# A decoder layer in split float32 on one core: two of seven Strassen operands formed later, half of the input's norm on GpSimd, the last product in two passes, no padded blocks in attention

## The chip, the cores and the metric

One core of a Trainium2 chip. The metric is device time in microseconds of one execution of the whole program. Rows of the profile come from one profiled execution. Engines: PE is TensorE (PEld its weight loads), DVE is VectorE, ACT is ScalarE, POOL is GpSimd, SP is SyncE, which here only issues DMAs.

## The reference

A decoder layer on 1024 tokens of width 1024 with 16 meta tokens ahead of them, all in float32:

```python
h = concatenate([meta, x])
h = h + 0.5 * rms_norm(swiglu(rms_norm(h, g_ffn1_pre), w_ffn1_in, w_ffn1_out), g_ffn1_post)
u = rms_norm(h, g_mix_pre)
q, k, v, f_logit, c_b, c_c, c_in, gate_a, gate_c = split_cols(u @ w_in)
# 8 heads of 64, causal, logits q.k/8 + F[t] - F[s], F = cumsum(log_sigmoid(f_logit + b_forget))
y_attn = forgetting_attention(q, k, v, log_f) @ w_attn_branch
y_conv = (c_b * short_conv(c_c * c_in, conv_w)) @ w_conv_branch
mixed = (sigmoid(gate_a) * y_attn + sigmoid(gate_c) * y_conv) @ w_out
h = h + rms_norm(mixed, g_mix_post)
h = h + 0.5 * rms_norm(swiglu(rms_norm(h, g_ffn2_pre), w_ffn2_in, w_ffn2_out), g_ffn2_post)
return h[16:]
```

`swiglu(x, w_in, w_out)` is `(silu(a) * b) @ w_out` with `a, b` the halves of `x @ w_in`; the hidden width is 2816, 22 tiles of 128.

## The kernel before, in words

**Numbers.** Every float32 operand is split into a high part `h`, rounded to the fp32r format by a ScalarE copy, and a low part `l`, the rest, by a VectorE subtraction (`split_into`, L138). A product is three matmuls, h·h, h·l and l·h, accumulated in PSUM (`mm3`, L142 to L146). So most matmuls of the trace stand on lines 144 to 146 and most vector work on lines 139 and 140, whatever the stage; the tiles' names tell the stage.

**Strassen products.** The two feed-forward blocks multiply by a scheme of seven products of half size (Strassen-Winograd). The input side has the operands B11, B21 (the first half of the tokens, first and second half of the channels), B22 (second half) and the sums T1 to T4. T2, T3 and T1 are differences of B22, B12 and B11; T4 = B21 - T2.

**Opening of the first block** (L389 to L456). Nine blocks of tokens come in (block 0 is the 16 meta tokens, 1 to 4 the first half, 5 to 8 the second). `norm_x` (L414) squares and sums on ScalarE (L421), takes the power -1/2 on GpSimd (L188), multiplies by the norm and the gain on VectorE (L426, two operations of 512 columns per block) and transposes on TensorE (L429) into two PSUM banks. For blocks 5 to 8 `sums_split` (L240) copies the second bank out (L252), forms the sums on VectorE (L253 to L256) and puts T2, T3, T1, then T4 (L261, L262) and B22 as h and l into their slots, block by block. The transposes of these four blocks share two PSUM banks (`psS`), so a block's transposes wait until the T1 and T3 of the one before are read.

**`ffn_in`** (L270) runs the 22 tiles. `first` makes P1 and P2 with B11 and B21; for tiles 0 to 2 it runs ahead of everything else. `rest` (L344) forms the tile's weight sums on VectorE (`load_rest`, L316) and makes P6 with T2, P7 with T3, P5 with T1, calls `late()` if there is one and this is tile 0 (L357), then makes P4 with T4 and P3 with B22. P1, P2, P6 and P4 of the first block also take the 16 meta tokens: 24 matmuls of 264 columns; P7, P5 and P3 are 12 of 512.

**Opening of the second block** (L1022 to L1067). The output projection of the mixer runs in two halves of tokens; the second half goes through `sums_split` with `t4=False`, and T4 is formed whole in `late` (L1057), two channel pairs at a time, when tile 0 reaches it.

**Attention** (L897 to L978). Per head, the queries are taken as four pairs of 128. `softmax` (L897) makes the weights of one tile of queries; for the first of a pair it sets the 128 columns behind its last key to zero (L918, GpSimd), so that both have the same length. `values` (L921) takes two key blocks of both query tiles at a time: four transposes of 128x128 into a bank (L935), the split, and per key block two matmuls of 256 columns (L943, L945), h and l. Other matmul work, gates and branches, is woven in between (`fill_work`).

**The last product** (L1147 to L1184). The second feed-forward block's output is again seven products, here with the tokens on the output side. P4 is the last: 11 steps in 6 batches; `prep2` (L1102) loads A's raw part and B's raw part, forms B's difference with a running sum R (L1121), and splits both. 11 x 4 x 3 = 132 matmuls of 512 columns fill four accumulators, `drain2` (L1145) adds them to the output, and `finish` (L1163) takes four tiles of 128 tokens: load the residual into one of two buffers `hr` (L1168), square and sum (L1171), scale (L1174), add (L1176, two halves), store.

**Order.** The program is written in order of data; the framework orders each engine's instructions by a simulated schedule with priorities (blocks under `tc.high_priority()` first). Each engine then runs its own list in that order, and SP and ACT issue their DMAs in order.

Of the kernel before, what the change touches and what calls it, by code (L numbers as in the profile page):

```python
# [13 lines left out]
P = 128  # L14
D = 1024
# [52 lines left out]
def hybrid_layer(ctx, tc, x, meta, w_in, b_forget, conv_w, w_attn, w_conv, w_out,  # L68
# [171 lines left out]
    def sums_split(bk, pt, e, ca, cb, t4=True):  # L240


        at = lambda b: bk[b].at(ALLP, ALLP, cb if b in ("T1", "T3", "B22") else ca)
        t1, t3 = pt
        b22, t2 = e

        def put(b, src):
            d = at(b)
            split_into(d.h, d.l, src)

        b11, b21 = at("B11"), at("B21")
# [4 lines left out]
        V.tensor_sub(t2, b22, t1)  # L256
# [149 lines left out]
    SLOTS = {"B11": (0, 1), "B21": (2, 3), "T2": (4, 5), "T3": (6, 7), "T1": (8, 9), "T4": (10, 11), "B22": (12, 13)}  # L406
# [7 lines left out]
    def norm_x(i):  # L414
# [9 lines left out]
        for q in range(2):  # L424
# [13 lines left out]
    for b in ("T2", "T3", "T1", "T4", "B22"):  # L438
        bk1[b] = operand(SLOTS, b, META, "u1")

# [17 lines left out]
    ffn_in(bk1, META, w1_in, g1d, loc, psD, psS, ahead, "w")  # L458
# [438 lines left out]
    def softmax(h, qt, fb):  # L897
# [19 lines left out]
        if qt % 2 == 0:  # L917
            G.memset(p[:, nk:nk + P], 0.0)  # L918
        return p

    def values(h, qp, pr, v):  # L921
# [97 lines left out]
    SLOTS2 = {"B11": (4, 5), "B21": (9, 0), "T3": (12, 6), "B22": (3, 10), "T4": (13, 11)}  # L1019
    bk2 = {b: operand(SLOTS2, b, 0, "u2") for b in ("B11", "B21")}  # L1020
    bk2["T1"], bk2["T2"] = mix[0, 0], mix[0, 1]
    for c, half in enumerate(TH):  # L1022
        if c:
            for b in ("T3", "B22"):
                bk2[b] = operand(SLOTS2, b, 0, "u2")

# [13 lines left out]
        def leave(i, w):  # L1040
# [6 lines left out]
            else:  # L1047
                sums_split(bk2, pts, halves(w[0]), cs, cs, t4=False)
# [6 lines left out]
    bk2["T4"] = operand(SLOTS2, "T4", 0, "u2")  # L1055

    def late():  # L1057
        for k in range(0, 4, 2):
            ks = slice(k, k + 2)
            t = loc["s"].page(f"t4_{k}")[:, :D].rearrange("p (k t) -> p k t", k=2)  # L1060
            b21, t2, t4 = (bk2[b].at(ALLP, ks) for b in ("B21", "T2", "T4"))
            V.tensor_sub(t, f32(b21.h), f32(t2.h))
            V.tensor_add(t, t, f32(b21.l))
            V.tensor_sub(t, t, f32(t2.l))
# [143 lines left out]
```

## Time and profile before

| | |
|---|---|
| runs | 2257.91, 2255.77, 2257.63 us; median 2257.63 |
| the profiled execution's own time | 2256.17 us |
| its span, first to last instruction | 2254.2 us |
| granted TensorE clock, mean | 0.974 of full speed |
| TensorE busy | 2122.8 us, 11622 matmuls |
| VectorE busy | 1434.2 us, 2332 instructions |
| ScalarE, GpSimd busy | 775.1 us, 103.8 us |

How to read it: times are in us from the span's start. A busy TensorE is not one at its peak, since matmuls are pipelined and their ends are modelled; the time from one matmul's start to the next one's start is what it occupies. Idle time of an engine is put down to what released it last, in brackets behind the instruction that follows.

### The profile page before, as it was taken

To read this page: it belongs to the slowest core of one execution; us is meant where nothing else is said; L and a number is where in the kernel's file an instruction comes from. 1 tells how busy PE (TensorE), PEld (TensorE's weight loads), DVE (VectorE), ACT (ScalarE), POOL (GpSimd) and SP (SyncE) were. 2 spreads that over 40 slices of the span, in tenths; PEclk is the share of its full clock that TensorE was granted. 3 is DMA by queue.
4 is the path that set the end of the run, shared out by engine and by line. 5 is a ranking of instruction groups with operands and counts; after the bars stand their busy time and mean duration, and the time that the engine had idled before them with its cause. 6 is when DMAs were issued, how large, how long until landed. Compare 5 with 4: busy or idle time off the path is not lost.

```text
span 2254.2 us, 30020 instructions
## 1 busy us (share of the span) xinstructions
PE 2122.8 (94%) x11622; PEld 1843.3 (82%) x11622; DVE 1434.2 (64%) x2332; ACT 775.1 (34%) x1269; POOL 103.8 (5%) x194
## 2 busy tenths in 40 slices
PE   5899999999998999999999999899799999999995
PEld 5799999989886998888888787688588888878874
DVE  7866666655968733345554457656876666648875
ACT  5322222223334421134343335334322222224432
POOL 1000000000001100000000001000000000000000
PEclk9899999999999999999999999899899999999997
DMA  4322222267557542343434183843142222278672
GB/s 132 103 85 85 85 74 75 88 236 240 189 166 225 183 125 71 97 113 95 128 107 117 63 230 120 261 138 113 51 125 80 80 82 83 82 254 277 200 259 98
DMA packets 275462, 305.44 MB, mean 136 GB/s; under 512 B 12812, under 2 KB 181848, under 8 KB 275320
## 3 DMA queue, kind: packets, MB, share of 16 engines
q1 hardware_dynamic: 239568, 242.94, 35.7%
q10 hardware_dynamic: 35720, 60.59, 7.7%
q8 instruction: 91, 1.49, 0.3%
q14 instruction: 51, 0.42, 0.1%
q0 software_dynamic: 32, 0.00, 0.0%
HBM read 233.47 MB, written 57.36 MB: 129 GB/s over the span
## 4 chain that ended last, share of the span: by engine, by line
PE 78%; DMA 9%; DVE 8%; ACT 2%; issue 2%; SPq 1%; POOL 0%; ACTq 0%; DVEq 0%; POOLq 0%
PE wP L144 6%; PE wP L145 6%; PE wP L146 6%; PE vP L144 6%; PE vP L145 6%; PE vP L146 6%; PE pg L144 2%; PE pg L145 2%; PE pg L146 2%; PE 2P L145 2%; PE 2P L146 2%; PE P L145 2%; PE 2P L144 2%; PE P L146 2%; PE P L144 2%
## 5 line engine op out<-in xcount | busy, mean ns | idle before, releaser
L145 PE MATMUL P<-blP,ahP 128*128 128x264 f32 (+1 forms) x452 | 146.4, 326 | 4.1 <-DVE ms_m0b L186 2.8
L144 PE MATMUL P<-bhP,ahP 128*128 128x264 f32 (+1 forms) x452 | 136.3, 320 | 9.7 <-ACT bhP L139 6.8
L146 PE MATMUL P<-bhP,alP 128*128 128x264 f32 (+1 forms) x452 | 145.3, 324 | 0.0
L145 PE MATMUL 2P<-lb2P,ha2P 128*128 128x512 f32 x308 | 122.0, 396 | 6.4 <-DVE lb2P L140 6.4
L146 PE MATMUL 2P<-hb2P,la2P 128*128 128x512 f32 x308 | 121.2, 395 | 0.0
L144 PE MATMUL 2P<-hb2P,ha2P 128*128 128x512 f32 x308 | 113.1, 394 | 6.0 <-ACT hb2P L139 3.7
L144 PEld LDWEIGHTS P<-bhP,ahP 128*128 128x128 f32 x452 | 84.3, 191 | 16.4 <-ACT bhP L139 7.8
L145 PEld LDWEIGHTS P<-blP,ahP 128*128 128x128 f32 x452 | 87.8, 194 | 11.7 <-DVE blP L140 6.0
L146 PEld LDWEIGHTS P<-bhP,alP 128*128 128x128 f32 x452 | 87.6, 194 | 5.6
L140 DVE TENSOR_TENSOR hbc<-tp,hbc 128x512 fp32r<-128x512 f32 (+1 forms) x112 | 67.1, 609 | 23.8 <-ACT hbc L139 23.1
L139 ACT CAST hbc<-tp 128x512 fp32r<-128x512 f32 (+1 forms) x112 | 56.8, 525 | 62.6 <-PE tp L935 57.2
L145 PEld LDWEIGHTS 2P<-lb2P,ha2P 128*128 128x128 f32 x308 | 58.8, 191 | 20.1 <-DVE lb2P L140 7.9
L144 PEld LDWEIGHTS 2P<-hb2P,ha2P 128*128 128x128 f32 x308 | 58.4, 190 | 19.1 <-ACT hb2P L139 4.1
L146 PEld LDWEIGHTS 2P<-hb2P,la2P 128*128 128x128 f32 x308 | 58.9, 191 | 12.6 <-DVE la2P L140 0.3
L909 PE MATMUL sc<-k,q 128*128 128x392 f32 (+6 forms) x224 | 56.3, 345 | 6.3 <-DMA k<-ha 2.9
L914 ACT ACTIVATE p<-p,mn 128x1040 f32<-128x1040 f32 (+3 forms) x64 | 50.5, 790 | 30.4 <-DVE mn L910 26.6
L144 PE MATMUL wP<-u1T4h,w 128*128 128x264 f32 x176 | 51.3, 291 | 4.6 <-ACT w L139 4.6
L144 PE MATMUL pg<-um0h,g_h 128*128 128x512 f32 x128 | 50.9, 398 | 2.1 <-ACT gt L836 2.1
L144 PE MATMUL pg<-um1h,g_h 128*128 128x512 f32 x128 | 51.5, 403 | 0.7 <-DVE ha L886 0.4
L144 PE MATMUL wP<-u1T2h,ws32h 128*128 128x264 f32 x176 | 51.0, 291 | 1.1 <-ACT u1T2h L139 1.1
L145 PE MATMUL wP<-u1T2l,ws32h 128*128 128x264 f32 x176 | 50.8, 289 | 0.8 <-DVE u1T2l L140 0.8
L145 PE MATMUL wP<-u1T4l,w 128*128 128x264 f32 x176 | 51.1, 290 | 0.0
(777 smaller groups left out, 6741.8 us busy)
## 6 DMA issues: line engine op xcount, KB each, us to landing
arP<-in_w_ffn_out_dram SPq DMA_DIRECT2D x35, 512.0 KB
ra2P<-g2d SPq DMA_DIRECT2D x35, 512.0 KB
rb2P<-in_w_ffn_out_dram SPq DMA_DIRECT2D x35, 512.0 KB
wrb<-in_w_ffn_in_dram SPq DMA_DIRECT2D x22, 512.0 KB
vrb<-in_w_ffn_in_dram SPq DMA_DIRECT2D x22, 512.0 KB
g2d<-vuc ACTq DMA_DIRECT2D x44, 256.0 KB
brP<-g1d SPq DMA_DIRECT2D x20, 528.0 KB
wra<-in_w_ffn_in_dram SPq DMA_DIRECT2D x19, 512.0 KB
```

The source lines that it names most:

```text
L139: S.copy(h, src)
L140: (eng or V).tensor_sub(l, src, f32(h))
L144: mm(o, a.h, b.h, start=start, stop=False)
L145: mm(o, a.h, b.l, start=False, stop=False)
L146: mm(o, a.l, b.h, start=False, stop=stop)
L909: mm(sc[:, :ke - k0], q[:, s, qt * P:qt * P + P], k[:, k0:ke], start=s == 0, stop=s == 1)
L914: S.activation(p[:, :nk], p[:, :nk], AF.Exp, bias=low, scale=-1.0, accum_out=mn[:, 3:4])
```

## The change

Four edits.

1. T4 and B22 of both feed-forward blocks are formed by a new function `last_sums`, which `ffn_in` calls where it called `late`: in tile 0, after P5. B22's raw values are kept in one float32 slot until then. The first block's T4, and its part for the meta tokens, leave the opening.
2. For blocks 5 to 8 the gain is multiplied in by GpSimd, one product of 128x1024 per block, and the norm by a ScalarE copy with a scale; VectorE's two operations per block go.
3. The last product P4 runs in two passes of two accumulators. Each pass loads its 256 columns of A; B's difference stays in R from the first pass and is split again in the second. After each pass `finish` takes its two tiles.
4. `softmax` no longer sets columns to zero. In `values` the key block that lies behind the first tile of queries gets one transpose, for the second tile alone, and its two matmuls take 128 columns; the split takes 384 columns there instead of 512.

The diff, cut to its core:

```diff
-        S.copy(b22, t3)
-        V.tensor_sub(t3, b22, t1)
+        S.copy(e22, t3)
+        V.tensor_sub(t3, e22, t1)
...
         put("T2", t2)
         put("T3", t3)
         put("T1", t1)
-        if t4:
-            V.tensor_sub(t2, f32(b21.h), t2)
-            V.tensor_add(t2, t2, f32(b21.l))
-            put("T4", t2)
-        put("B22", b22)
+
+    def last_sums(bk, slots, nm, off, raw, loc):
+        b22 = bk["B22"] = operand(slots, "B22", off, nm)
+        for k in range(0, 4, 2):
+            ks = slice(k, k + 2)
+            split_into(b22.h[:, ks], b22.l[:, ks], raw[:, ks])
+        bk["T4"] = operand(slots, "T4", off, nm)
+        for k in range(0, 4, 2):
+            ks = slice(k, k + 2)
+            t = loc["s"].page(f"{nm}t4_{k}")[:, :2 * (H + off)].rearrange("p (k t) -> p k t", k=2)
+            b21, t2, t4 = (bk[b].at(ALLP, ks) for b in ("B21", "T2", "T4"))
+            V.tensor_sub(t, f32(b21.h), f32(t2.h))
+            V.tensor_add(t, t, f32(b21.l))
+            V.tensor_sub(t, t, f32(t2.l))
+            split_into(t4.h, t4.l, t)
...
         r = rstd(sh[:, 0:1], f"x{i}")
-        for q in range(2):
+        if i > 4:
+            G.tensor_mul(xt, xt, gb)
+            S.activation(xt, xt, AF.Copy, scale=r)
+        for q in range(2 if i < 5 else 0):
...
-        sums_split(bk1, norm_x(i), halves(xts[i]), slice(o, o + P), slice(o - META, o - META + P))
+        cb = slice(o - META, o - META + P)
+        sums_split(bk1, norm_x(i), (b22f[:, :, cb], halves(xts[i])[1]), slice(o, o + P), cb)
...
-    ffn_in(bk1, META, w1_in, g1d, loc, psD, psS, ahead, "w")
+    ffn_in(bk1, META, w1_in, g1d, loc, psD, psS, ahead, "w",
+           lambda: last_sums(bk1, SLOTS, "u1", META, b22f, loc))
...
-        if qt % 2 == 0:
-            G.memset(p[:, nk:nk + P], 0.0)
...
+            at = lambda j, s: slice(256 * j + P * s, 256 * j + P * s + P)
+            first_s = {2 * qp + 2: 1}
+            hi = 0
             for j, b in enumerate(blks):
                 k0 = META + P * (b - 1)
-                for s in range(2):
-                    nc.tensor.transpose(tp[:, j, s * P:s * P + P], pr[s][:, k0:k0 + P] if b else pmet[:, s],
-                                        ident)
+                for s in range(first_s.get(b, 0), 2):
+                    c = at(j, s) if b <= 2 * qp + 1 else at(j, 0)
+                    nc.tensor.transpose(tp[:, c], pr[s][:, k0:k0 + P] if b else pmet[:, s], ident)
+                    hi = c.stop
...
+            split_into(pth[:, :hi], ptl[:, :hi], tp[:, :hi])
             for j, b in enumerate(blks):
                 vv = vb[:, b - 1, :] if b else vm
-                mm(po, vv, pth[:, j], start=first_mm, stop=False)
+                s = first_s.get(b, 0)
+                o, c = po[:, P * s:], slice(256 * j, 256 * j + 256 - P * s)
+                mm(o, vv, pth[:, c], start=first_mm, stop=False)
                 first_mm = False
-                mm(po, vv, ptl[:, j], start=False, stop=b == 0)
+                mm(o, vv, ptl[:, c], start=False, stop=b == 0)
...
+    def last_product(j):
+        ps = psQ(f"2P4_{j}")
+        cols = slice(2 * P * j, 2 * P * j + 2 * P)
+        for k0, nk in batches(2):
+            nm = f"P4{j}_{k0}"
+            with tc.high_priority():
+                l, raw, h = (tile2("a", x, nk, f"{x}a{nm}", False, 2 * P) for x in "lrh")
+                load(raw, a2_src(1, 1, k0, nk, cols))
+                split_into(h, l, raw)
+                a = Split(h, l)
+                R = runB(k0, nk)
+                if j == 0:
+                    b = prep2("b", "P4", k0, nk)
+                else:
+                    l, h = (tile2("b", x, nk, f"{x}b{nm}", False) for x in "lh")
+                    split_into(h, l, R)
+                    b = Split(h, l)
+            for k in range(nk):
+                for m in range(2):
+                    mm3(ps[m], a.at(ALLP, k, slice(m * P, m * P + P)), b.at(ALLP, k),
+                        start=k0 + k == 0, stop=k0 + k == FH - 1)
+        for m in range(2):
+            drain2("P4", 2 * j + m, ps[m])
...
-    product2("P4")
-    finish(1)
+    for j in range(2):
+        last_product(j)
+        finish(1, (2 * j, 2 * j + 1))
```

Left out are the second block's call of `last_sums`, the slots' numbers (B22's raw values take the slot that T4's low part gets afterwards) and the removal of `late` and of `product2`'s argument `groups`.

## Rows read from the trace of the kernel before

**Rows 1.** The page's busy times, shares of the span and instruction counts by engine.
```profile
PE 2122.8 (94%) x11622; PEld 1843.3 (82%) x11622; DVE 1434.2 (64%) x2332; ACT 775.1 (34%) x1269; POOL 103.8 (5%) x194
```
**Rows 2.** Busy time by stretch: PE, PEld, DVE, ACT, POOL; clock, DMA share, GB/s.
```profile
50.00:100.00 50.00, 37.23 (x182) 32.91 (x183) 44.66 (x69) 18.04 (x27) 1.74 (x4) 0.76 0.29 85
...
1000.00:1050.00 50.00, 49.96 (x273) 42.79 (x273) 28.55 (x81) 22.58 (x47) 5.54 (x12) 1.00 0.31 91
...
1600.00:1650.00 50.00, 43.35 (x182) 35.30 (x181) 45.95 (x62) 16.70 (x22) 0.00 (x0) 0.90 0.28 85
...
2200.00:2254.00 54.00, 31.60 (x131) 25.17 (x129) 31.40 (x44) 11.69 (x23) 3.45 (x4) 0.78 0.25 86
```
**Rows 3.** Order of time, PE, first opening: start, us, instruction, [idle before, releaser].
```profile
65.89 0.59 PE L144 MATMUL wP<-u1T4h,w 128*128 128x264 f32 x1 [4.61 <-ACT w L139]
...
75.09 0.77 PE L144 MATMUL wP<-u1T3h,ws32h 128*128 128x512 f32 x1 [4.49 <-DVE u1T3l L140]
```
**Rows 4.** DVE to 100 us by form (us, mean ns, idle), then one of time.
```profile
L426 DVE SCALAR_TENSOR_TENSOR xt<-xt,r_x,gb 128x512 f32<-128x512 f32 x18 | 12.7, 749 | 1.3 <-POOL r_x L188 1.3
...
L140 DVE TENSOR_TENSOR u1T4l<-xt,u1T4h 128x512 fp32r<-128x512 f32 x4 | 2.7, 686 | 1.4 <-ACT u1T4h L139 1.4
...
L140 DVE TENSOR_TENSOR u1B22l<-xt,u1B22h 128x512 fp32r<-128x512 f32 x4 | 2.7, 680 | 0.0
...
78.40 0.69 DVE L140 TENSOR_TENSOR u1T1l<-xps,u1T1h 128x512 fp32r<-128x512 f32 x1
```
**Rows 5.** Order of time, PE, attention: 256 columns, transposes, 512 columns, 16 columns.
```profile
1046.75 0.28 PE L943 MATMUL pv<-hbc,vbuf 128*128 128x256 f32 x1
1046.87 0.28 PE L945 MATMUL pv<-hbc,vbuf 128*128 128x256 f32 x1
...
1047.46 1.04 PE L935 MATMUL tp<-ident,p 128*128 128x128 f32 x8
1048.25 0.48 PE L145 MATMUL pg<-um1l,g_h 128*128 128x512 f32 x1
...
1084.10 0.39 PE L146 MATMUL pqk<-um1h,k_l 128*128 128x512 f32 x1
1084.33 0.28 PE L909 MATMUL sc<-k,q 128*128 128x16 f32 x2
1084.52 0.50 PE L144 MATMUL pg<-um0h,g_h 128*128 128x512 f32 x1
```
**Rows 6.** Order of time, DVE, `late` of the second block: two operations of one line.
```profile
1608.48 2.35 DVE L1062 TENSOR_TENSOR t<-u2B21h,mix01h 128x1024 f32<-128x1024 f32 x2
```
**Rows 7.** Order of time: GpSimd operations alone and beside VectorE.
```profile
1050.07 0.46 POOL L902 TENSOR_TENSOR fbuf<-fbuf,rows 128x128 f32<-128x128 f32 x1 [1.35 <-DVE mn L910]
...
1002.09 1.22 DVE L140 TENSOR_TENSOR g_l<-g_r,g_h 128x1024 fp32r<-128x1024 f32 x1
...
1002.25 1.38 POOL L902 TENSOR_TENSOR fbuf<-fbuf,rows 128x128 f32<-128x128 f32 x1 [0.69 <-DVE mn L910]
...
2006.95 3.65 POOL L194 TENSOR_SCALAR g2post<-g2post 128x1024 f32<-128x1024 f32 x1 [416.15 <-DMA RB<-in_w_ffn_out_dram]
...
2009.05 1.23 DVE L140 TENSOR_TENSOR lb2P<-rb2P,hb2P 128x1024 fp32r<-128x1024 f32 x1 [0.23 <-ACT hb2P L139]
```
**Rows 8.** The last product and the tail: PE in order of time, DVE by form.
```profile
2204.73 0.80 PE L145 MATMUL 2P<-lb2P,ha2P 128*128 128x512 f32 x1 [3.85 <-DVE lb2P L140]
2205.32 0.63 PE L146 MATMUL 2P<-hb2P,la2P 128*128 128x512 f32 x1
2205.75 0.63 PE L145 MATMUL 2P<-lb2P,ha2P 128*128 128x512 f32 x1
...
2235.06 0.39 PE L146 MATMUL 2P<-hb2P,la2P 128*128 128x512 f32 x1
...
L1176 DVE TENSOR_TENSOR y<-y,hr 128x512 f32<-128x512 f32 x8 | 5.1, 686 | 3.3 <-DMA hr<-h2d 3.3
L1174 DVE SCALAR_TENSOR_TENSOR y<-y,r_o,g2post 128x1024 f32<-128x1024 f32 x4 | 5.0, 1281 | 0.7 <-POOL r_o L188 0.7
```

More of the change, by code (lines that the diff above doesn't have):

```diff
@@ L236, in staggered, with sums_split @@
         leave(*last)
[L240 to L243 removed]
+    def sums_split(bk, pt, e, ca, cb):
+        at = lambda b: bk[b].at(ALLP, ALLP, cb if b in ("T1", "T3") else ca)
         t1, t3 = pt
[L245 removed]
+        e22, t2 = e
         def put(b, src):
@@ L437, in hybrid_layer @@
             split_into(d.h, d.l, pt[q][:, :, :wd])
-    for b in ("T2", "T3", "T1", "T4", "B22"):
+    for b in ("T2", "T3", "T1"):
         bk1[b] = operand(SLOTS, b, META, "u1")
+    b22f = blk4(13, H, "b22f", F32)
     m = slice(0, META)
@@ L1023, in hybrid_layer @@
         if c:
-            for b in ("T3", "B22"):
-                bk2[b] = operand(SLOTS2, b, 0, "u2")
+            bk2["T3"] = operand(SLOTS2, "T3", 0, "u2")
+            b22f = blk4(10, H, "b22f2", F32)
         def enter(i):
@@ L1047, in leave @@
             else:
-                sums_split(bk2, pts, halves(w[0]), cs, cs, t4=False)
+                sums_split(bk2, pts, (b22f[:, :, cs], halves(w[0])[1]), cs, cs)
         staggered(range(4), enter, leave)
@@ L1054, in hybrid_layer @@
     loc = {"s": Turns(0, 1), "4": Turns(2, 3), "uc": Turns(4, 5), "ps": Turns(6, 7, 8, 9)}
[L1055 to L1064, printed above, removed]
-            split_into(t4.h, t4.l, t)
-    ffn_in(bk2, 0, w2_in, g2d, loc, psO, psA, ahead, "v", late)
+    ffn_in(bk2, 0, w2_in, g2d, loc, psO, psA, ahead, "v",
+           lambda: last_sums(bk2, SLOTS2, "u2", 0, b22f, loc))
     psQ = Turns(*range(8)).bank2
@@ L1145, in drain2 @@
                 V.tensor_add(c21, c21, ps)
-    def product2(pr, groups=1):
-        bs = {}
-        for mg in range(groups):
-            mms = range(mg * 4 // groups, (mg + 1) * 4 // groups)
-            ps = {m // 2: psQ(f"2{pr}_{m}") for m in mms if m % 2 == 0}
-            for k0, nk in batches(2):
-                if mg == 0:
-                    bs[k0] = prep2("a", pr, k0, nk), prep2("b", pr, k0, nk)
-                a, b = bs[k0]
-                for k in range(nk):
-                    for m in mms:
-                        mm3(ps[m // 2][m % 2], a.at(ALLP, k, slice(m * P, m * P + P)), b.at(ALLP, k),
-                            start=k0 + k == 0, stop=k0 + k == FH - 1)
-            for m in mms:
-                drain2(pr, m, ps[m // 2][m % 2])
@@ L1163, in finish, with product2 @@
-    def finish(half):
-        for m in range(4):
+    def product2(pr):
+        ps = [psQ(f"2{pr}_{j}") for j in range(2)]
+        for k0, nk in batches(2):
+            a, b = prep2("a", pr, k0, nk), prep2("b", pr, k0, nk)
+            for k in range(nk):
+                for m in range(4):
+                    mm3(ps[m // 2][m % 2], a.at(ALLP, k, slice(m * P, m * P + P)), b.at(ALLP, k),
+                        start=k0 + k == 0, stop=k0 + k == FH - 1)
+        for m in range(4):
+            drain2(pr, m, ps[m // 2][m % 2])
@@ new lines, in last_product @@
+    def last_product(j):
+        ps = psQ(f"2P4_{j}")
+        cols = slice(2 * P * j, 2 * P * j + 2 * P)
+        for k0, nk in batches(2):
+            nm = f"P4{j}_{k0}"
[11 more added lines that the diff above has]
+                    b = Split(h, l)
+            for k in range(nk):
+                for m in range(2):
+                    mm3(ps[m], a.at(ALLP, k, slice(m * P, m * P + P)), b.at(ALLP, k),
+                        start=k0 + k == 0, stop=k0 + k == FH - 1)
+        for m in range(2):
+            drain2("P4", 2 * j + m, ps[m])
@@ L1165, in finish @@
+    def finish(half, ms=range(4)):
+        for m in ms:
             ti = 4 * TH[half] + m
```

31 lines of the change are left out of this document (12 added, 19 removed).

## The prediction, written before the changed kernel ran

> **What bounds the kernel now.** I read the page's busy shares first. TensorE works 94% of the span [rows 1], so a gain can only come from the 6% in which it stands still or runs slowly, or from matmul work that is left out. Next I read busy time by stretches of 50 us: in most stretches TensorE is nearly full, and in the ones the change touches it is not [rows 2]. In the opening of the first feed-forward block (50 to 100 us) TensorE works 37.2 us at a granted clock of 0.76, beside a VectorE at 44.7. The opening of the second (1600 to 1650) has 43.4 beside 46.0. The end (2200 to 2254) has 31.6 at 0.78. So in both openings VectorE is what TensorE waits for. Then I read the order of time there. TensorE's two longest waits after 60 us end on work behind the input sums: 4.6 us before the weights of tile 1, 4.5 us before T3 of the last block [rows 3]. VectorE finishes that block's T1, its last operand of the first three, at 78.4 + 0.7 = 79.1 us [rows 4].
>
> **Part 1, the opening.** Ahead of those 79.1 us VectorE loses three things [rows 4]. The gain-and-norm of blocks 5 to 8 is 8 operations of 0.75 = 6.0 us. The low halves of B22 are 4 x 0.68 = 2.7. T4 of blocks 5 to 7 (that of block 8 comes later anyway) is 3 x 3 operations of 0.69 = 6.2. Together 14.9 us; operations overlap by a tenth in the queue, so I count 13. Two costs stand against it. P4 now needs all of T4, so the 24 matmuls with T4 that filled TensorE's waits (12 of tile 0, 12 of tile 1 from 65.9 us on [rows 3]) come later: 24 x 0.12, by the narrow row [rows 5], = 2.9 us. And `last_sums` is 2 operations of 1.22 for B22 and 8 of some 1.25 for T4 (1024 and 1056 elements; a pair of such takes 2.35 [rows 6]), 12.4 us on VectorE, and tile 1's weight sums stand behind it. What covers it is tile 0's other products: P6 24 x 0.12 and P7, P5, P3 12 x 0.23 each [rows 5], 11 us together, against 12.4 and some 3 us of evictions. That leaves about 2.5 us of waiting and tile 1 starts late. Net: -13 + 2.9 + 2.5 = **-7.6 us**. If the cover holds fully it is -10. If the blocks keep their rhythm because each needs both PSUM banks of the transposes, whatever VectorE does, nothing is won and the costs stay: +5.
>
> **Part 2, GpSimd.** The trace has no GpSimd product of 128x1024; one of 128x128 takes 0.46 us [rows 7], so eight times that, 3.7 us, is a ceiling, 14.7 for four blocks on an engine that is nearly idle here. From below I take 0. The first block's product lies on the way to its transposes, while TensorE still has the first products of tiles 0 to 2; the other three run while VectorE works on the block before, 7 operations of 0.69 = 4.8 us. ScalarE gets one scaling copy of 1024 elements per block and gives B22's and T4's roundings to `last_sums`; it has the time. I count nothing. What could make it cost: a GpSimd product took 1.38 in place of 0.46 when VectorE had begun a 1.22 us subtraction of two SBUF operands just before it; but a VectorE subtraction of the same kind that began while GpSimd was in the middle of a 3.65 us scaling took its usual 1.23 [rows 7]. So in these rows GpSimd gives way, VectorE does not. The Trainium skill (SBUF — State Buffer, section SBUF: two separate sides) states it harder: the port pair is an exclusive lock, whoever starts first holds it for the whole instruction, and the other blocks fully. The trace agrees for the first direction (1.38) and not for the second (1.23). By that rule the products could hold VectorE up; this is one of the rivals below.
>
> **Part 3, the second opening.** T4 was formed late already. B22's low halves leave the blocks (one of 0.68 lies on the last block's chain) and come back as 2.4 us ahead of T4's pairs [rows 6]. TensorE has P6, P7, P5 to do meanwhile; I count +1, between -0.7 and +1.8.
>
> **Part 4, attention.** In each of 32 pairs of query tiles one transpose goes: eight follow each other in 1048.25 - 1047.46 = 0.79 us [rows 5], so 32 x 0.099 = 3.2 us on TensorE, which is the bound here (50.0 of 50 us from 1000 to 1050 [rows 2]). 64 matmuls shrink from 256 to 128 columns. The trace has no such width: the same matmul at 256 columns comes every 0.12 us, and two of 16 columns take 1084.52 - 1084.33 = 0.19, 0.095 each, so hardly less [rows 5]. From above I bound it by a matmul of 512 columns, 0.23 (four passes over 128 columns), in case a narrow one is not streamed once. Change per matmul: -0.025 to +0.11; in sum -1.6 to +7.0. I take the nearest row, the same operation at 256: 0. GpSimd's 32 fills and a quarter of 32 roundings on ScalarE and VectorE go too; they lie beside TensorE's work and I count nothing. **-3.2 us**.
>
> **Part 5, the last product.** The last matmul ends at 2235.06 + 0.39 = 2235.45; the span ends 18.8 us later. In it VectorE does 4 evictions and 8 additions of 0.69 and 4 scalings of 1.28 (13.4 us) and waits 3.3 us for rows of `hr` that cannot load before a buffer is free [rows 8]. With two tiles done under the second pass, half the work (6.7) and the waits (3.3) leave the tail: -10. Against it stands VectorE's supply. A batch of the first pass needs 1.22 for B's difference, 1.22 for its low half, 0.69 for A's half: 5.5 batches x 3.13 = 17.2 us against 66 x 0.227 = 15.0 of matmuls; the pass may end 2.2 late. The second pass needs 5.5 x 1.91 = 10.5, because B is rounded again, and 6.7 for the first two tiles: 17.2 against 15.0, another 2.2. Queues: SP issues 12 loads of A of 256 KB in place of 6 of 512 KB, and stores of the first two tiles now stand among them, each behind an addition; loads behind a store wait for it, but they are due only one batch later. **-5.6 us**, from -9 (all hidden) to +4 (nothing won, both delays paid).
>
> **Sum.** -7.6 + 1 - 3.2 - 5.6 = -15.4 on the profiled execution's 2256.2 us (its span is 2254.2, so 2 us lie around it): 2240.8. The median of the three runs is 1.5 above the profiled one: **2242 us**.
>
> **Rivals.** (a) The narrow matmuls cost a 512-column slot: +7, 2249. For: nothing narrower than 256 of this kind is on record except 16, whose slot an LDWEIGHTS could set. Against: the 16-column row shows no penalty. (b) The opening wins nothing, because the sums keep their rhythm or because each GpSimd product holds VectorE's operands for up to 3.7 us, 14.7 for four, which eats the 13 us: 2250. Against: the 1.23 beside a running GpSimd [rows 7]. (c) The first two tiles are not finished under the second pass, VectorE being booked for 17.2 of 15 us, so the change doesn't do what it says: 2248. (d) Slower: in the first pass each batch asks VectorE for 3.13 us per 2.7 us of matmuls, TensorE halts at every batch, and its clock stays at the lower level. After the 3.85 us wait before this product a matmul took 0.63 where 0.39 is usual; its slot was 2205.75 - 2205.32 = 0.43 for 0.23 [rows 5, 8]. All 132 matmuls that way cost 26 us: 2268. It decides from about 100 slow matmuls on (0.2 x 100 = 20 = 15.4 + 4.5). Against: a halt of 0.4 us per batch is a tenth of the one that is followed by slow matmuls.
>
> **Chances.** Forecast 0.45; (a) 0.24; (b) 0.10; (c) 0.06; two of (a) to (c) together 0.10, 2255 to 2257; (d) 0.05. A measurement of this kernel tells 0.2%, 4.5 us, from no change. Faster by more: the forecast and (a) to (c) singly, 0.85. Within: the pairs, 0.10. Slower: 0.05. The range takes the good ends (-10, -0.7, -4.8, -9, which is 2233) and (a) to (c) singly: 2232 to 2254.
>
> **What would show it.** In the profile after, T1 of the last block should end at 64 to 68 us in place of 79, and P7 of tile 0 follow it; if T1 moves and steady matmuls don't start earlier, `last_sums` ate it. The 128-column row gives its price by its spacing. GpSimd's products should take 2 to 4 us and VectorE beside them its usual 0.68. From the last matmul to the end should be 9 to 12 us, with no wait for `hr`, and that matmul should end at most 4 us later against the start of the product than now. The forecast is wrong if the clock in the last product is low, if TensorE waits for T4 more than 5 us, or if the 128-column slot is 0.2 or more.

## The result, and the profile after

The changed kernel takes 2244.47 us (median of four runs, 2240.33 to 2245.74) against 2257.77 for the kernel before, measured again beside it: a ratio of 0.9937, 95% interval 0.992 to 0.9954, 13.3 us less. The prediction said 2242 and 2232 to 2254. The sum came out; two of its five terms did not. Two single executions far from all others, one of run e4 below (2939 us at a granted clock of 0.68) and one of the kernel before (9114 us), are left out of the medians and ratios.

The page's busy times of the changed kernel, as [rows 1], and four stretches of 50 us (the last shorter), as [rows 2]:

```profile
PE 2116.9 (95%) x11590; PEld 1836.9 (82%) x11590; DVE 1438.7 (64%) x2328; ACT 781.0 (35%) x1278; POOL 104.2 (5%) x162
```
```profile
50.00:100.00 50.00, 38.52 (x215) 33.21 (x215) 45.61 (x66) 18.95 (x27) 1.53 (x4) 0.86 0.24 69
1000.00:1050.00 50.00, 49.25 (x277) 41.99 (x275) 28.36 (x84) 23.64 (x51) 4.17 (x9) 1.00 0.31 91
1600.00:1650.00 50.00, 50.00 (x212) 40.67 (x211) 46.84 (x63) 14.10 (x16) 0.00 (x0) 0.96 0.37 111
2200.00:2238.00 38.00, 26.89 (x118) 21.92 (x118) 29.63 (x44) 13.52 (x24) 4.04 (x4) 0.92 0.35 120
```

The first opening still leaves TensorE idle or slow (38.5 of 50 us, 37.2 before); the second and the end are better filled, and the end at a higher granted clock (0.92, 0.78 before). VectorE is no less busy than it was.

Where did the time go? I took the start of the last matmul of each stage in both profiled runs and subtracted. The first input product is taken to its last matmul with T4 (the last matmuls with B22 follow 2.6 us later in every run): 489.8 before, 487.6 after, 2.2 us won. The output product behind it, counted from there, whose code the change doesn't touch: 2.2 more. Attention, from its first projection to its last value product: 471.6 and 468.5, 3.1. The rest of the mixer 1.1. The second block's opening 0.5 (0.8 up to its first product, 0.3 lost in the products). The last seven products: 0.5 lost. The tail behind the last matmul's start: 19.1 and 12.0, 7.1. Together 15.7, the difference of the spans; it is 2.4 more than that of the medians, since the profiled run of the changed kernel was its fastest.

The first opening, TensorE in order of time, as [rows 3]:

```profile
61.83 1.08 PE L444 MATMUL xps<-ident,xt 128*128 128x128 f32 x4 [3.81 <-DVE u1T3l L140]
66.08 1.09 PE L444 MATMUL xps<-ident,xt 128*128 128x128 f32 x4 [3.17 <-DVE u1T1l L140]
...
73.05 0.63 PE L144 MATMUL wP<-u1T3h,ws32h 128*128 128x512 f32 x1
```

and VectorE, then GpSimd, as [rows 4] and [rows 7]:

```profile
24.50 4.16 DVE L434 TENSOR_TENSOR sh_x<-sh_x 128x1 f32<-128x1 f32 x3
31.47 3.53 DVE L441 SCALAR_TENSOR_TENSOR xt<-xt,r_x,gb 128x512 f32<-128x512 f32 x2
35.52 2.25 DVE L434 TENSOR_TENSOR sh_x<-sh_x 128x1 f32<-128x1 f32 x1
39.89 0.68 DVE L254 TENSOR_TENSOR xps<-b22f,xps 128x512 f32<-128x512 f32 x1
...
65.94 2.36 DVE L140 TENSOR_TENSOR u1B22l<-b22f,u1B22h 128x1024 fp32r<-128x1024 f32 x2
73.72 2.42 DVE L273 TENSOR_TENSOR u1t<-u1B21h,u1T2h 128x1056 f32<-128x1056 f32 x2
76.39 0.68 DVE L140 TENSOR_TENSOR u1T1l<-xps,u1T1h 128x512 fp32r<-128x512 f32 x1
```
```profile
23.92 4.72 POOL L437 TENSOR_TENSOR xt<-xt,gb 128x1024 f32<-128x1024 f32 x2 [1.39 <-ACT sq L433]
31.59 2.86 POOL L437 TENSOR_TENSOR xt<-xt,gb 128x1024 f32<-128x1024 f32 x1
35.38 2.38 POOL L437 TENSOR_TENSOR xt<-xt,gb 128x1024 f32<-128x1024 f32 x1
```

Three things are to be seen. T1 of block 8 ends at 76.39 + 0.68 = 77.1, where 64 to 68 was predicted. TensorE waits 3.8 and 3.2 us, not with products but with the transposes of block 8, for T3 and T1 of block 7: they need the two PSUM banks that these read. And VectorE's first three rows are far too long: three operations on one column, 0.16 each, take 4.16 us, from just behind the start of GpSimd's two products to just after their end (28.64 and 28.66); two scalings of 0.71 take 3.53, beside a product that runs to 34.45; a single column takes 2.25, to 37.77, and the product beside it ends at 37.76. Over their usual lengths that is 3.7 + 2.1 + 2.1 = 7.9 us of standing still, for 6.0 us of work taken off it.

In attention, TensorE in order of time, as [rows 5]:

```profile
1059.78 0.22 PE L960 MATMUL pv<-hbc,vbuf 128*128 128x128 f32 x1
1059.84 0.27 PE L962 MATMUL pv<-hbc,vbuf 128*128 128x128 f32 x1
1059.95 0.33 PE L960 MATMUL pv<-hbc,vbuf 128*128 128x256 f32 x1
1060.12 0.28 PE L962 MATMUL pv<-hbc,vbuf 128*128 128x256 f32 x1
1060.24 0.28 PE L960 MATMUL pv<-hbc,vbuf 128*128 128x256 f32 x1
1060.36 0.28 PE L962 MATMUL pv<-hbc,vbuf 128*128 128x256 f32 x1
1060.48 0.38 PE L951 MATMUL tp<-ident,pmet 128*128 128x128 f32 x2
```

The narrow matmuls come 0.06 and 0.11 us apart, but the 256-column one behind them keeps its slot for 0.17: 1060.12 - 1059.78 = 0.34 for the three, against 1060.48 - 1060.12 = 0.36 for three of 256. In all 32 such pairs the medians are 0.06, 0.11 and 0.17. So narrowing is worth 0.02 per pair, 0.6 us over 32.

The tail, all engines in order of time, as [rows 8]:

```profile
2222.11 1.29 DVE L1202 TENSOR_TENSOR y<-y,hr 128x512 f32<-128x512 f32 x2
2223.92 1.29 DVE L1202 TENSOR_TENSOR y<-y,hr 128x512 f32<-128x512 f32 x2
2226.47 1.28 DVE L1151 TENSOR_TENSOR y<-y,2P 128x512 f32<-128x512 f32 x2 [1.27 <-PE 2P L146]
2226.50 0.39 PE L146 MATMUL 2P<-hbP,laP 128*128 128x512 f32 x1
...
2232.01 2.49 DVE L1202 TENSOR_TENSOR y<-y,hr 128x512 f32<-128x512 f32 x4
```

The first two tiles' additions stand ahead of the last matmul, and no row waits for `hr`. From the last matmul's end (2226.89) to the last addition's (2234.50) it is 7.6 us. Before it was 15.4, from 2235.45 to the end of this row:

```profile
2249.54 1.29 DVE L1176 TENSOR_TENSOR y<-y,hr 128x512 f32<-128x512 f32 x2 [1.22 <-DMA hr<-h2d]
```

### The profile page after: what moved, and what is told of

It reads as the page before. It is cut to its first block, busy times and chain, and to the rows that moved or that the text cites. A ratio compares the mean times of both kernels' runs of the same rounds, so it can differ in the third digit from the quotient of the medians.

```text
span 2238.5 us, 29941 instructions
## 1 busy us (share of the span) xinstructions
PE 2116.9 (95%) x11590; PEld 1836.9 (82%) x11590; DVE 1438.7 (64%) x2328; ACT 781.0 (35%) x1278; POOL 104.2 (5%) x162
## 4 chain that ended last, share of the span: by engine, by line
PE 80%; DMA 8%; DVE 7%; issue 2%; ACT 1%; SPq 1%; POOL 0%; ACTq 0%; POOLq 0%; DVEq 0%
PE wP L144 6%; PE wP L146 6%; PE wP L145 6%; PE vP L144 6%; PE vP L146 6%; PE vP L145 6%; PE pg L144 3%; PE pg L145 2%; PE pg L146 2%; PE P L145 2%; PE P L146 2%; PE P L144 2%; PE 2P L145 2%; PE 2P L146 2%; PE 2P L144 2%; DMA arP<-in_w_ffn_out_dram 2%
## 5 line engine op out<-in xcount | busy, mean ns | idle before, releaser
L145 PE MATMUL 2P<-lb2P,ha2P 128*128 128x512 f32 x264 | 103.8, 393 | 2.4 <-DVE lb2P L140 2.3
L146 PE MATMUL 2P<-hb2P,la2P 128*128 128x512 f32 x264 | 103.4, 393 | 0.0
L144 PE MATMUL 2P<-hb2P,ha2P 128*128 128x512 f32 x264 | 95.9, 392 | 2.5 <-ACT ha2P L139 2.1
L140 DVE TENSOR_TENSOR hbc<-tp,hbc 128x512 fp32r<-128x512 f32 (+2 forms) x112 | 62.9, 572 | 19.6 <-ACT hbc L139 18.5
L139 ACT CAST hbc<-tp 128x512 fp32r<-128x512 f32 (+2 forms) x112 | 52.9, 494 | 59.3 <-PE tp L951 55.9
L927 ACT ACTIVATE p<-p,mn 128x1040 f32<-128x1040 f32 (+3 forms) x64 | 50.6, 790 | 36.0 <-DVE mn L923 30.7
L145 PEld LDWEIGHTS 2P<-lb2P,ha2P 128*128 128x128 f32 x264 | 49.9, 189 | 14.7 <-DVE lb2P L140 4.3
L146 PEld LDWEIGHTS 2P<-hb2P,la2P 128*128 128x128 f32 x264 | 50.0, 190 | 10.5 <-DVE la2P L140 0.3
L915 POOL TENSOR_TENSOR fbuf<-fbuf,rows 128x128 f32<-128x128 f32 x64 | 31.3, 489 | 585.8 <-DVE mn L923 481.6
L923 DVE CUSTOM_DVE_ANT_0 p<-sc,fbuf 128x16 f32<-128x16 f32 (+3 forms) x64 | 28.5, 451 | 43.1 <-PE tp L951 30.0
L146 PE MATMUL wP<-u1T2h,ws32l 128*128 128x264 f32 x176 | 50.4, 288 | 2.0 <-DVE ws32l L140 2.0
```

The costliest lines, as they stand in the source:

```text
L139: S.copy(h, src)
L140: (eng or V).tensor_sub(l, src, f32(h))
L144: mm(o, a.h, b.h, start=start, stop=False)
L145: mm(o, a.h, b.l, start=False, stop=False)
L146: mm(o, a.l, b.h, start=False, stop=stop)
L915: G.tensor_add(fb[:, nk - P:nk], fb[:, nk - P:nk], mask)
```

## The experiments

Two theories for the first opening. **Rhythm**: a block's sums wait for the block before to leave the two PSUM banks, so work taken off VectorE is not time won. **Hold**: GpSimd's products stop VectorE, so they cost what they were to save. Their rivals: the long rows are a coincidence; VectorE is simply full; the late sums stand in the way.

All twelve runs, in one table. "T1" is the end of the last block's T1, "input" the start of the first input product's last matmul with T4 (T2 in e6), "attention" the stretch as above, all in the profiled run. The times come from four sets of runs (changed; e1 to e4; e5 to e8; e9 to e12), each beside runs of the kernel before, so between sets the ratios are to be compared.

| run | T1 | input | attention | time, us | ratio to before (95%) |
|---|---|---|---|---|---|
| before | 79.1 | 489.8 | 471.6 | 2257.8 | |
| changed | 77.1 | 487.6 | 468.5 | 2244.5 | 0.9937 (0.992 to 0.9954) |
| e1 changed, no GpSimd product | 77.3 | 487.8 | 469.7 | 2248.0 | 0.996 (0.9946 to 0.9974) |
| e2 before + GpSimd products | 82.6 | 492.5 | 476.0 | 2264.4 | 1.0033 (1.002 to 1.0046) |
| e3 changed, products in pieces | 75.2 | 485.7 | 469.1 | 2241.1 | 0.9931 (0.9918 to 0.9944) |
| e4 before + late sums | 76.9 | 487.4 | 475.1 | 2257.5 | 1.0002 (0.9991 to 1.0014) |
| e5 e3 + more banks | 65.6 | 481.8 | 469.4 | 2232.7 | 0.9898 (0.9883 to 0.9914) |
| e6 changed, no late work | 83.8 | 490.7 | 471.1 | 2236.8 | 0.9913 (0.9895 to 0.993) |
| e7 changed, no gain | 78.3 | 489.4 | 470.2 | 2244.9 | 0.9956 (0.9941 to 0.9972) |
| e8 before + attention edit | 79.2 | 489.2 | 469.4 | 2255.2 | 0.9995 (0.9984 to 1.0006) |
| e9 changed + more banks | 68.0 | 483.5 | 468.3 | 2238.6 | 0.9914 (0.9901 to 0.9927) |
| e10 e1 + more banks | 66.1 | 480.4 | 467.3 | 2234.5 | 0.99 (0.9887 to 0.9913) |
| e11 before + more banks | 64.1 | 482.8 | 474.4 | 2255.8 | 0.9984 (0.9971 to 0.9997) |
| e12 e5, half the products | 64.4 | 480.9 | 467.7 | 2234.9 | 0.9909 (0.9895 to 0.9923) |

### The GpSimd products: taken out, put in alone, cut up

```diff
-        if i > 4:
-            G.tensor_mul(xt, xt, gb)
-            S.activation(xt, xt, AF.Copy, scale=r)
-        for q in range(2 if i < 5 else 0):
+        for q in range(2):
```

> The changed kernel with the gain and norm of blocks 5 to 8 back on VectorE (two operations of 0.75 us per block), all else as changed. Theory 'hold': in the changed kernel VectorE stands still while a GpSimd product of 128x1024 runs (4.16 us for three operations of 0.16, 3.53 for 1.42, 2.25 for 0.15: 7.9 us over), which is more than the 6.0 us of work it was spared. Then without it the rows of VectorE before 40 us have their usual lengths, the sums of block 5 begin near 36 us (39.9 in the changed kernel), T1 of block 8 ends 2 to 5 us earlier than 77.1, and the time is 2 to 5 us below the changed kernel: 2239 to 2243. Rival 'coincidence': VectorE's long rows only show that it waited for something else; then the 6.0 us come on top: 2246 to 2251, T1 of block 8 at 79 to 83.

The time, 2248.0, is in the range of the rival "coincidence"; T1 is in neither range. VectorE's rows have their usual lengths and the sums of block 5 begin at 34.8, as "hold" said, but T1 ends at 77.3, as in the changed kernel: the five us gained at the start are lost again before block 8. So the long rows are no coincidence, but taking the products out won nothing here. The input product ends alike (487.8). The total is 3.5 us worse by the medians. Of the 10.0 us between the two profiled runs (the slowest of e1, the fastest of the changed kernel) 6.7 lie in the output product behind it, the same code (269.9 and 263.2); whether the medians differ by it too no trace shows.

The same lines the other way round, in the kernel before:

> The kernel before with GpSimd's gain products for blocks 5 to 8 as the only edit. Theory 'hold': VectorE is spared 6.0 us and held 7.9: the sums of block 5 begin at 39 to 41 us in place of 35.5 and the time is the same or worse, 2257 to 2262. Rival 'coincidence' (and the prediction's own sum, which took 6.0 us off VectorE for nothing): T1 of block 8 ends near 73 to 75 in place of 79.1 and the time is 4 to 6 us below before: 2252 to 2254.

"Hold": the sums begin at 40.1 and T1 ends at 82.6, 3.5 later; 2264.4, slower than expected even so. Of the 8.2 us between the two profiled runs the opening accounts for 2.7 (the input product); 4.5 lie in attention (476.0, 471.6 before), which the edit doesn't touch.

```diff
-            G.tensor_mul(xt, xt, gb)
+            for c in range(0, D, P):
+                G.tensor_mul(xt[:, c:c + P], xt[:, c:c + P], gb[:, c:c + P])
```

> The changed kernel with each GpSimd product of 128x1024 cut into eight of 128x128 (0.46 us each by the one row of the kernel before). If the engine that comes first holds the other for the whole of an instruction, VectorE gets in after each piece: its operations of 128x1 beside the products take under 0.8 us each where 1.4 to 2.25 were seen, the stalls before 40 us fall from 7.9 to about 3, and the time is 1 to 4 us below the changed kernel (2240 to 2243), though GpSimd's products end later. If the two share a rate instead, VectorE's rows stay as long in sum and the time stays within 2 us of the changed kernel.

2241.1, in the range of "hold", with T1 and the input product 1.9 us before those of the changed kernel. The total alone would not tell the two apart: the ratios are 0.9931 and 0.9937, and their intervals overlap. GpSimd and VectorE of this kernel in order of time:

```profile
23.55 8.22 POOL L438 TENSOR_TENSOR xt<-xt,gb 128x128 f32<-128x128 f32 x16 [0.77 <-ACT sq L433]
...
26.46 0.68 DVE L140 TENSOR_TENSOR u1B21l<-xps,u1B21h 128x512 fp32r<-128x512 f32 x1
27.38 1.59 DVE L140 TENSOR_TENSOR wa_l<-wa_r,wa_h 128x1024 fp32r<-128x1024 f32 x1 [0.24 <-ACT wa_h L139]
...
33.65 0.41 DVE L434 TENSOR_TENSOR sh_x<-sh_x 128x1 f32<-128x1 f32 x1
```

A piece is 8.22 / 16 = 0.51 us. An operation with two operands in SBUF waits for at most one piece: a column 0.41 in place of 0.15, a subtraction 1.59 in place of 1.22. One that reads PSUM (`xps`) takes its usual 0.68 in the middle of the pieces. That is a hold per instruction, not a shared rate.

### The late sums alone, and what the late work and the gain cost

```diff
-    ffn_in(bk1, META, w1_in, g1d, loc, psD, psS, ahead, "w")
+    ffn_in(bk1, META, w1_in, g1d, loc, psD, psS, ahead, "w",
+           lambda: last_sums(bk1, SLOTS, "u1", META, b22f, loc))
```

with the other lines of edit 1, on the kernel before:

> The kernel before with the late forming of T4 and B22 in both feed-forward blocks as the only edit. By the prediction's terms without the GpSimd part (VectorE loses 2.7 + 6.2 us ahead of T1 of block 8, 8 counted with overlap; +2.9 for the P4 matmuls that filled waits, +2.5 for the wait on the late sums, +1 for the second opening): 8 - 2.9 - 2.5 - 1 = 1.6 us won, 2256, T1 of block 8 at 70 to 72. Rival 'order': the late sums are ready data, so B22's low half (2.4 us), T4's first subtractions (2.4) and tile 1's weight sums stand ahead of T1 of block 8 on VectorE, T1 ends after 75 and nothing is won: 2257 to 2260. Rival 'rhythm': what the changed kernel won in the openings (2.2 us by the last matmul of the first block's input product) came from here alone and GpSimd ate more: 4 us or more won, 2253 or less.

T1 ends at 76.9 and the total is unchanged (1.0002): the rival "order" by both numbers. The input product still ends 2.4 us earlier, all that the changed kernel has.

```diff
-           lambda: last_sums(bk1, SLOTS, "u1", META, b22f, loc))
+           lambda: bk1.update(T4=bk1["T2"], B22=bk1["T3"]))
```

> The changed kernel without the forming of T4 and B22 of the first feed-forward block: P4 takes T2 and P3 takes T3 in their place, so that part of the computation is left out (some 12.4 us of VectorE). Theory 'order': the late sums stand on VectorE ahead of and among the work that TensorE waits for (2.4 us of B22 and 2.4 of T4 before T1 of block 8 ends), so without them T1 of block 8 ends at 71 to 73 in place of 77.1 and the last matmul of the first input product starts 4 to 8 us earlier than 487.6: 2237 to 2241. Rival, the prediction's cover: TensorE's other products of tile 0 hide the late sums but for 2.5 us; then at most 2 to 3 us are won: 2242 to 2243.

A miss for both in the trace. This profile runs 3.5 us late before any instruction that the edit touches (GpSimd's power for block 3 at 25.54, 21.99 in the changed kernel); with that taken off T1 ends at 80.3 and the input product at 487.2. So leaving the late work out brings T1 no earlier, which speaks for "rhythm". The time of 2236.8 comes from elsewhere: the output product took 256.1 us here, 7.1 less than in the changed kernel. Of these, 4.6 are one wait of TensorE near its start, for the input product's last eviction: it takes 2.7 to 4.9 us in the other thirteen profiles and is missing in this one. VectorE has that eviction in its list behind a low half of the output product's, which it makes in the changed kernel 9.0 us after the last matmul with T4, in e6 1.4 us after. Its row in the changed kernel, then in e6:

```profile
496.53 1.26 DVE L140 TENSOR_TENSOR blP<-brP,bhP 128x1056 fp32r<-128x1056 f32 x1 [7.49 <-ACT bhP L139]
```
```profile
492.14 1.26 DVE L140 TENSOR_TENSOR blP<-brP,bhP 128x1056 fp32r<-128x1056 f32 x1
```

In e6 alone SP issues the load for it (`brP`) ahead of those of the running sums (`RA`, `RB`). So I put these 4.6 us down to the order of the loads, and not to the sums that are left out; no run tests it. Why the framework ordered them so is open, and so are the other 2.5.

```diff
-            G.tensor_mul(xt, xt, gb)
```

> The changed kernel without the gain of blocks 5 to 8 (the GpSimd products are left out, and with them that part of the computation; the norm by ScalarE stays). Theory 'hold': VectorE's 7.9 us of standing still go; the sums of block 5 begin at 34 to 36 us in place of 39.9, T1 of block 8 ends at 72 to 74, and 3 to 5 us are won: 2239 to 2242. Rival: the products were off the way (the prediction counted them at nothing): 2243 to 2246.

The sums begin at 37.4, T1 ends at 78.3, and the time is the rival's, 2244.9. VectorE is freed of the 7.9 us and T1 does not move: the products were off the way after all, but only because something else held T1.

### The bank wait itself

```diff
-        pt = pt or [psS(f"xps{i}_{q}") for q in range(2)]
+        pt = pt or [(psS if i % 2 else psD)(f"xps{i}_{q}") for q in range(2)]
```

On the kernel with pieces:

> The kernel with the gain in eight pieces, and the transposes of blocks 6 and 8 in the six PSUM banks that the first products use, so that a block no longer waits until T1 and T3 of the one before are read. Theory 'rhythm': the blocks' sums begin 9 to 10 us apart because of that wait, whatever VectorE is spared; with the wait gone two blocks' sums run together, T1 of block 8 ends 5 to 10 us before the 75.2 of the kernel with pieces, and the last matmul of the first input product starts 2 to 6 us before its 485.7: 2235 to 2239. Rival 'VectorE': VectorE is full between 40 and 85 us and only the order of its work changes; T1 of block 8 may end earlier but the first products come later by as much, since they now share their banks: 2240 to 2244, or later.

2232.7, better than either theory had it: the fastest kernel here, 1.0% below before. Its 50 to 100 us and VectorE's last T1:

```profile
50.00:100.00 50.00, 46.04 (x276) 41.72 (x275) 47.64 (x71) 19.66 (x28) 2.38 (x5) 0.93 0.31 89
```
```profile
47.38 0.69 DVE L254 TENSOR_TENSOR xps<-b22f,xps 128x512 f32<-128x512 f32 x1
49.51 0.69 DVE L254 TENSOR_TENSOR xps<-b22f,xps 128x512 f32<-128x512 f32 x1
...
64.89 0.68 DVE L140 TENSOR_TENSOR u1T1l<-xps,u1T1h 128x512 fp32r<-128x512 f32 x1
```

The sums of two blocks now begin 2 us apart, T1 ends at 65.6, and the input product ends 8.0 us before that of the kernel before. That is the size of the -7.6 that the prediction gave to the change, but not its cause: with the banks alone (e11, below) 7.0 of it come without any work taken off VectorE.

On the changed kernel, on it without GpSimd products, and on the kernel before:

> The changed kernel with only the transposes of blocks 6 and 8 moved to the other six PSUM banks; the GpSimd products stay whole. Theory 'rhythm plus hold': the bank wait goes (no transposes of block 8 behind T1 and T3 of block 7), T1 of block 8 ends 8 to 11 us before 77.1, but VectorE's 7.9 us beside the products stay: the last matmul of the first input product starts 3 to 6 us before 487.6, and the time is 2236 to 2240, above the 2232.7 of the kernel that has pieces too. Rival 'pieces alone': the gain of that kernel came from the pieces and their order; then 2242 to 2245.

> The changed kernel with more banks and the gain and norm of blocks 5 to 8 back on VectorE: no GpSimd product at all. Theory 'hold': VectorE gets 6.0 us of work and is freed of 7.9, so it is no slower than the same with whole products: 2234 to 2239, T1 of block 8 at 64 to 69. Rival: once the bank wait is gone VectorE alone is the bound, and the 6.0 us count in full against the kernel with pieces: 2238 to 2241.

> The kernel before with more banks alone. Theory 'both are needed': with T4 and B22 formed in the blocks, VectorE has 14.9 us more ahead of T1 of block 8 than with the late sums; the bank wait goes but VectorE is full: T1 ends at 74 to 78 in place of 79.1 and 0 to 4 us are won: 2252 to 2257. Rival 'the banks are all': the bank wait alone set the opening, and 6 to 9 us are won without any of the change: 2247 to 2250.

The first two came as the theories said: 2238.6 with T1 at 68.0, and 2234.5 with T1 at 66.1. VectorE of e9, order of time:

```profile
24.65 4.10 DVE L434 TENSOR_TENSOR sh_x<-sh_x 128x1 f32<-128x1 f32 x3
31.57 3.50 DVE L441 SCALAR_TENSOR_TENSOR xt<-xt,r_x,gb 128x512 f32<-128x512 f32 x2
35.59 2.23 DVE L434 TENSOR_TENSOR sh_x<-sh_x 128x1 f32<-128x1 f32 x1
```

The hold is there as before, and now that the banks no longer hide it, whole products cost 4.1 us more than none by the medians (2238.6 and 2234.5; the intervals of the ratios overlap, but the input product too ends 3.1 us later) and 3.6 to 5.9 more than pieces (e5, by the ratios and by the medians; e5 ran beside other runs of before).

e11 went against me in the opening: with T4 and B22 still formed in the blocks, T1 ends at 64.1 and the input product 7.0 us earlier. So the bank wait set when T1 came. VectorE had not stood still meanwhile: between 50 us and T1 it idled 3.1 us in the kernel before, and in e11 it doesn't idle at all between 40 us and T1. What changed is the order of its work. In e11 weight sums of tiles 0 and 1, most of which stood ahead of T1 in the kernel before, come behind it:

```profile
63.45 0.68 DVE L140 TENSOR_TENSOR u1T1l<-xps,u1T1h 128x512 fp32r<-128x512 f32 x1
64.39 0.68 DVE L328 TENSOR_TENSOR ws<-wrb 128x512 f32<-128x512 f32 x1
66.80 1.22 DVE L140 TENSOR_TENSOR ws32l<-ws,ws32h 128x1024 fp32r<-128x1024 f32 x1
```

From its start to T1's end VectorE is busy 60.6 us in the kernel before and 50.6 in e11. So T1 comes 15.0 us earlier and the input product, which needs the weight sums too, 7.0. Of these 7.0 us only 2 to 4 are in the total (2255.8, 2257.9 for before beside it; ratio 0.9984); in its profile the output product (268.9, 265.4 before) and attention (474.4, 471.6) took longer. What gives the time back there is not settled.

```diff
-        if i > 4:
+        if i > 6:
...
-        for q in range(2 if i < 5 else 0):
+        for q in range(2 if i < 7 else 0):
```

> The kernel with pieces and more banks, but with GpSimd's gain only for blocks 7 and 8; blocks 5 and 6 are back on VectorE (3.0 us). In the kernel with pieces the power -1/2 of block 4 stood on GpSimd behind 8.2 us of products of blocks 5 and 6, VectorE waited 1.6 us for it and TensorE 8.3 us for block 4's transposes. Theory 'queue': with those products gone the power comes at once, the transposes of block 4 start before 29 us in place of 33.3, and the time is 1 to 4 us below 2232.7: 2229 to 2232. Rival: the 3.0 us on VectorE eat that: 2232 to 2235.

The transposes of block 4 do start at 27.9, and nothing is won: 2234.9. TensorE in order of time:

```profile
27.91 2.79 PE L445 MATMUL xps<-ident,xt 128*128 128x128 f32 x12 [3.03 <-ACT sq L433]
...
35.42 0.59 PE L144 MATMUL wP<-u1B11h,wa_h 128*128 128x264 f32 x1 [1.02 <-DVE u1B11l L140]
```

The products begin 1.9 us before those of e5 (35.42, 37.28), but at the lower clock: the granted clock is 0.50 of full speed from 35.4 to 38.7 us and they come 0.22 us apart, where in e5 it is 1.00 from 37.3 us on and they come 0.12 apart. The second product starts at 40.57, in e5 at 40.37.

### The attention edit alone

```diff
-                for s in range(2):
+                for s in range(first_s.get(b, 0), 2):
...
-                mm(po, vv, pth[:, j], start=first_mm, stop=False)
+                mm(o, vv, pth[:, c], start=first_mm, stop=False)
```

with the rest of edit 4:

> The kernel before with the attention edit alone. The prediction's term: 32 transposes of 0.099 us go, 64 narrow matmuls change nothing: -3.2 us, 2254 to 2255, and the narrow pairs' slots leave the spacing of the group as it is (two of 128 and the next take 0.34 where three of 256 take 0.35). Rival 'more than TensorE': the roundings of 512 columns that shrink to 384 and the fills that go shorten the chain that the products wait for, since TensorE shows waits for them (2 us each on the high and low halves): -4 to -6 us, 2251 to 2253. Rival 'price': a narrow matmul costs a slot of 0.23 as in the prediction's rival (a): +3 to +4, 2261.

The total can't tell (0.9995, 0.9984 to 1.0006). The stretch can a little: 469.4, 2.2 less than in the one profile of the kernel before. Over all profiles the ten with this edit have 467.3 to 471.1 (mean 469.1), the four without 471.6 to 476.0 (mean 474.3). The rival "price" is out.

## Why the prediction was right in the sum and wrong in two terms

**Part 1: -7.6 predicted, -2.2 measured.** The step that failed is the first: that VectorE's work ahead of T1 is time. 13 us were taken off (or meant to be) and T1 moved by 2.0. The prediction named the reason, "if the blocks keep their rhythm because each needs both PSUM banks", and gave it a tenth; the 2250 of rival (b) also leaves out the costs of 5 that Part 1 adds to that case. It could have been followed one step further back in the trace of before, in order of time, VectorE and TensorE:

```profile
67.80 0.68 DVE L140 TENSOR_TENSOR u1T1l<-xps,u1T1h 128x512 fp32r<-128x512 f32 x1
69.55 1.06 PE L429 MATMUL xps<-ident,xt 128*128 128x128 f32 x4
71.26 0.70 DVE L253 TENSOR_TENSOR xps<-xt,xps 128x512 f32<-128x512 f32 x1
```

T1 of block 7 leaves its bank at 68.48, the last transposes of block 8 follow at 69.55, its first sum at 71.26: 2.8 us in which VectorE can do nothing for block 8. e5 and e11 show it: with the wait gone the opening wins 8.0 and 7.0 us, in e11 without any work taken off. Nor does work taken off VectorE come back as time: the gain's 6.0 us, taken off with no product beside VectorE (e7 against e1), won nothing (T1 78.3 and 77.3, input product 489.4 and 487.8). The late sums alone won 2.4 (e4 against before; with more banks e10 against e11 too). By number that is what their own terms add up to, 8 - 2.9 - 2.5 = 2.6, but T1 moved by 2.2 and not by 8, so the agreement is luck. One of the two long waits read in [rows 3] was misread besides. The 4.6 us before tile 1's weights end on a rounding of weights that had come by DMA, not on the input sums, and VectorE itself waits for that transfer:

```profile
65.22 0.69 DVE L328 TENSOR_TENSOR ws<-wrb 128x512 f32<-128x512 f32 x1 [0.95 <-DMA wrb<-in_w_ffn_in_dram]
```

In the changed kernel VectorE filled the freed time with work that was ready: B22's lows (2.36 at 65.94) and T4's first subtractions (2.42 at 73.72) again stand ahead of T1. Of the 2.5 us of waiting that the prediction counted for the late sums none stands at T4: no product waits for it over 1 us.

**Part 2: 0 predicted, 7.9 us of VectorE's standing still.** "GpSimd gives way, VectorE does not" was read from one row with a scaling on GpSimd [rows 7], which has one tensor operand; the products have two. The row itself was read rightly: the same subtraction begins inside the same scaling in all fourteen profiles and takes 1.22 or 1.23 us in each. The step that failed is carrying it over to products. That the number of operands makes the difference fits all these rows, but no run tested it by itself. The products' own length was as bounded, 2.36 to 2.86 of at most 3.7. The cost hid behind the bank wait (e1 and the changed kernel have the same T1) and shows without it: 4.1 us (e9, e10). The Trainium skill (SBUF — State Buffer, section SBUF: two separate sides) says that whoever starts first, GpSimd or a VectorE operation with two inputs in SBUF, holds the port pair for the whole instruction. For the products the trace agrees (2.25 us for a column of 0.15, and beside the pieces of e3 0.68 as usual where one input is in PSUM); for the scaling of [rows 7] it does not. As measured, the products made VectorE stand still for 7.9 us to spare it 6.0.

**Part 3: +1 predicted, -0.5 measured in the pair of profiled runs, -1.8 in the means.** TensorE's waits between 1552 and 1612 us, summed by what released them, of the kernel before and then of the changed one:

```profile
PE vP L144 <- DVE w L207: 9.8, 1, 9.8
PE vP L144 <- ACT mix01h L139: 5.0, 1, 5.0
PE n03u L224 <- DVE mix00l L140: 1.6, 1, 1.6
```
```profile
PE vP L144 <- DVE w L207: 9.4, 1, 9.4
PE vP L144 <- ACT mix01h L139: 4.0, 1, 4.0
PE n03u L224 <- DVE mix00l L140: 1.0, 1, 1.0
```

2.0 us less in sum, of which 0.8 are won at the first product with the blocks' sums. In all profiles with late sums the way from the start of the mixer's last matmul to the start of that product is 40.6 to 42.7 us (ten; mean 41.5), without 43.4 to 44.7 (four; 44.1); the products behind it take 400.0 (means) in place of 399.3. My reading, which no run here isolates: B22's low halves lay on more of the blocks' chain than the one of 0.68 that was counted, and TensorE's products covered most of the 2.4 us that they cost later.

**Part 4: -3.2 predicted, -3.1 measured** in the pair of profiled runs; taking the narrow matmul at 0 was right, 0.02 us a pair. The means give -5.2, which 32 transposes don't explain; that is left open.

**Part 5: -5.6 predicted, -6.6 measured**, out of two errors: the tail gave 7.1 instead of 10, and the product itself ended 0.5 later, not 4.4. Three of the four evictions counted into the tail (2.0 of 13.4 us) stood ahead of the last matmul's end already, which explains 1.0 of the 2.9 missing; the rest was not followed up. The tail is 11.8 to 12.3 us in each of the nine profiles with edit 3 and 19.0 to 19.5 in the five without, the surest gain here.

So the sum came out by luck: in the pair of profiled runs the miss of 5.4 in part 1 was covered by 1.5 of part 3, 1.0 of part 5 and 3.3 that the unchanged output product (2.2) and the rest of the mixer (1.1) happened to give. Rival (b) was right for the opening and wrong for the sum; (a), (c) and (d) didn't come.

## What to carry to other kernels

When the busiest engine is to be relieved ahead of a deadline, follow the deadline's chain back past that engine first: here the block before had to leave two PSUM banks, and one line about banks moved the input product by 7.0 us where 13 us of VectorE's work moved it by 2.2. A busy engine does not show what it is busy with: VectorE was nearly full while block 8 waited, with work that could have come later. A GpSimd product of two SBUF operands was not free beside VectorE here: cut it into pieces, or count its whole length as VectorE's. Splitting the last product so that half of its outputs are finished under the other half took some 7 us off the tail in every profile.

## What the runs showed of the hardware

VectorE's one-column operation took 2.25 us beside a whole GpSimd product and 0.41 beside pieces of 0.51, while operations with one operand in PSUM kept their 0.68 beside those pieces. A VectorE subtraction of two SBUF operands inside a GpSimd scaling of one kept its 1.23. A matmul of 128 columns had a slot of 0.06 to 0.11 us, but the next one paid back most of what it saved (0.34 and 0.36 for three). And unchanged code does not cost the same in every profile: the output product of the first block took 263.2 to 269.9 us, once 256.1, in fourteen profiles of fourteen kernels, a spread larger than most of the effects looked for here. Part of it is the program, as in e6; part is not, since before, e2 and e8 have the same order of matmuls and of loads there and took 265.4, 268.4 and 267.0.
